# A decoder step in fp32: spacing out the scan's activation and moving the first row tile's products

## Chip, cores and metric

One Trainium2 chip, one core. The time is microseconds of the device for one execution of the whole program; lower is better. TensorE (PE) does matrix products, PEld is its loading of weights, VectorE (DVE) and ScalarE (ACT) work element by element, GpSimd (POOL) and SyncE (SP) here issue transfers and little else. "line" numbers such as L905 are those of the kernel before; in the kernel after, the same code stands some lines lower.

## What is computed

One layer of a decoder for 304 rows (16 meta tokens, 256 prompt tokens, 8 x 4 sample tokens), width 2048, all in float32:

```python
x = x + 0.5 * swiglu(rmsnorm(x), ffn1)          # hidden 5632
z = rmsnorm(x) @ w_in                           # 2048 -> 1024 + 1024 + 2048 + 2048
a = pool_mix(z[:, :1024])                       # sliding means over 2, 4, 8, 16 rows, minus identity, then pool_w
s = gelu(s5_scan(z[:, 1024:2048]))              # 64 groups of 16 channels, 64 complex states each
s = s * sigmoid(s @ glu_w + glu_b)
m = sigmoid(gate_a) * (a @ w_branch_a) + sigmoid(gate_b) * (s @ w_branch_b)
x = x + m @ w_out
x = x + 0.5 * swiglu(rmsnorm(x), ffn2)
y = rmsnorm(x)
```

The scan is linear: bu = u times a complex matrix per group, then h[t] = lam * h[t-1] + bu[t], then the real part of h times a matrix, plus d * u. The gelu behind it is written as y * sigmoid(c * (y * y + k) * y).

## The kernel before

**Products and weights.** Each weight is split into a high and a low part (`whi` by ACT, `wlo` by DVE), each activation too, and each product is three matmuls (`mm3`, L249 to L251). Weights come in chunks of 512 KB on SP's queue, one chunk per step of `proj`: 24 matmuls for a chunk, then `step`. `step` makes the high part of a later chunk (`high`), runs what was posted for this place (`flush`), makes the low part, loads the next chunk, and then advances the side work: a generator that yields after each small step, `g.rate` steps per chunk (2.25 during the scan). So the program order on every engine follows from where in the chunks the side steps fall. Each engine runs its own queue in that order.

**PSUM.** Four banks serve the projections, three (`psaux`) the side work in turn, one (`pslong`) the scan's output and, at the start, some products.

**The mixer.** `w_in` is run in eight column pairs, in the order `COLS`: pairs 0 to 3 feed the pool mix (`Pool.run`, side work), pairs 4 to 7 are the scan's input u, the ssm projections. Then `mixed` multiplies by `pool_w`, then come eight gate and `w_branch_a` projections, then eight more gate projections. The scan runs as side work beside all of this.

**The scan.** `Scan.run` goes through eight row tiles i, each in two halves h of twelve steps n (`rows`, all DVE: products with the tables `ee`, two scans, products again). For a tile, `into` makes bu: one matmul of the stacked input `us` (high, low, high part) with `bs`, then a copy by ACT from the bank to a `row` tile; twelve matmuls and copies per tile, two per call. The calls for tile i + 1 are spread over tile i at steps 5, 8, 11, 14, 17 and 20, counted over both halves. For the first tile all twelve are made at the start of `run`, in three side steps. `stored` writes the split input to memory (`usc`), `stacked` reads it back as `us`, `matrices` reads `bs` and `cs`; all these are issued on POOL's queue, and `us` and `bs` have one buffer each, so a read waits for the products of the tile before. `outof` (step 3) makes the output `yps` of the tile before, and `act` its gelu: gy = d * u + yps (DVE), square (ACT), gw (DVE), sigmoid (ACT), gy * gw (DVE), the high part of it (ACT) and the low part (DVE).

In `run`, the gelu of the tile before is a generator that is advanced after the steps 6, 7 and 8:

```python
yield 1
if acts is not None and n >= 6 and next(acts, None) is None:
    acts = None
```

Of the kernel before, what the change touches and what calls it, by code (L numbers as in the profile page):

```python
# [10 lines left out]
F32 = mybir.dt.float32  # L11
F32R = mybir.dt.float32r
I32 = mybir.dt.int32
AF = mybir.ActivationFunctionType
ALU = mybir.AluOpType
# [27 lines left out]
JB = 2  # L43
# [4 lines left out]
LATE = 8  # L48
STIR = 9
LAG = 0  # L50
COLS = (0, 1, 2, 4, 3, 5, 6, 7)
ROWS = 12
MAGIC = 12582912.0
# [158 lines left out]
def vcol(g, name, i):  # L212
    c = VROWS[name][0] + i
    return g.vec[:, c:c + 1]
# [628 lines left out]
class Scan:  # L843
# [76 lines left out]
    def act(self, i):  # L920
        g, nc = self.g, self.g.nc
        y = g.act.tile([P, NT], F32, tag="acc", name=nm(g, "gy"))[:, :NL]
        w = g.act.tile([P, NT], F32, tag="gw", name=nm(g, "gw"))[:, :NL]
        nc.vector.scalar_tensor_tensor(y, self.u[i][:, NMETA:], vcol(g, "ssm_d", i), self.yps[i], ALU.mult, ALU.add)
        nc.scalar.activation(w, y, AF.Square)
        yield 1
        nc.vector.scalar_tensor_tensor(w, w, 1.0 / 0.044715, y, ALU.add, ALU.mult)
        nc.scalar.activation(w, w, AF.Sigmoid, scale=2.0 * 0.044715 * math.sqrt(2.0 / math.pi))
        yield 1
        nc.vector.tensor_tensor(y, y, w, ALU.mult)  # L930
        self.sparts.append(split(g, y, NL, "Y"))
        yield 1

    def rows(self, sb, s):

# [41 lines left out]
    def first(self):  # L977

        self.matrices(0)
        self.pair = [self.load(0), self.load(1)]  # L980

    def run(self):
        half = 4 // JB
        nb = NJ // JB
        pair = self.pair
        for ri in (2, 1, 0):
            for h in range(half):
                self.into(0, pair, ri, h, h == half - 1)
            yield 1
        self.stored(1)  # L990
        self.stacked(1)
        self.matrices(1, outs=False)
        done, acts = None, None
        for i in range(KW):
            nxt = [dict(bu={}) for _ in range(half)]
            for h in range(half):
                sb = i * half + h
                rows = self.rows(sb, pair[h])
                if sb >= 1 and sb + 1 < nb:
                    new = self.load(sb + 1)  # L1000
                    (nxt[0] if h else pair[1])["ee"] = new["ee"]
                for n, row in enumerate(rows):
                    row()
                    if h == 0 and n == 3 and done is not None:
                        self.outof(i - 1, done)
                        acts = self.act(i - 1)
                    if h == 0 and n == 8 and i + 1 < KW:
                        self.matrices(i + 1, ins=False)
                    k, late = divmod(h * len(rows) + n - 5, 3)
                    if i + 1 < KW and late == 0 and 0 <= k < 6:  # L1010
                        self.into(i + 1, nxt, 2 - k % 3, k // 3)
                    if h == 0 and n == 2 and i + 2 < KW:
                        self.stored(i + 2)
                    if h and n == 9 and i + 2 < KW:
                        self.stacked(i + 2)
                        self.matrices(i + 2, outs=False)
                    yield 1
                    if acts is not None and n >= 6 and next(acts, None) is None:
                        acts = None
            done, pair = pair, nxt  # L1020
        self.outof(KW - 1, done)
        yield 1
        yield from self.act(KW - 1)

    def store(self, O, sp):
        g, nc = self.g, self.g.nc
# [85 lines left out]
def mixer(g, norm, O, ps0):  # L1112
# [14 lines left out]
    with ExitStack() as cm:  # L1127
        g.mix = cm.enter_context(g.tc.tile_pool(name="mix", bufs=1))
        with ExitStack() as cs:
            sp = cs.enter_context(g.tc.tile_pool(name="scan", bufs=1))  # L1130
            scan = Scan(g, sp)
            pool = Pool(g, O)
            dparts, aparts = [], []
            g.side, g.rate = None, POOLRATE
            for p in COLS:
                if p < KW // 2:
                    pool.fetch(p)
                ps = proj(g, "w_in", p * 256, norm.x, NT, KD) if p else ps0
                if p < KW // 2:
                    more = lambda p=p, ps=ps: also(g, pool.run(p, ps, norm, dparts))  # L1140
                    g.post.append(more if p else lambda more=more: g.post.append(more))
                else:
                    g.post += [lambda q=q: scan.input(q, norm.r) for q in ps]
                if p == 1:
                    scan.first()
                if p == KW // 2 - 1:
                    nc.gpsimd.dma_start(O[3][0, :, :HIST - NS], g.I["state_pool"][0, :, NS:])
                if p == KW // 2 + 1:
                    drain(g)
                    g.side, g.rate = scan.run(), MIXRATE  # L1150
                    g.owed = -LAG * MIXRATE
            def mixed():
                for q in range(4):
                    if q % 2:
                        flush(g)
                    else:
                        wh, wl = g.w.take("pool_w", 2 * q, 4, 0)
                    for f in range(2):
                        ps = bank(g, "pw")[:, :NL]
                        for k in range(2):  # L1160
                            fs = slice(f * P, (f + 1) * P)
                            kk = 2 * (q % 2) + k
                            mm3(g, ps, wh[:, kk, fs], wl[:, kk, fs], dparts[2 * q + k], k == 0, k == 1)
                        g.post.append(lambda i=2 * q + f, ps=ps: aparts.append(
                            split(g, ps, NL, "Y", vcol(g, "pool_scale", i))))
                    if q % 2:
                        step(g)

            mixed()
            for p in range(KD // 2):  # L1170
                pg = proj(g, "w_in", 2 * WP + p * 256, live, NL, KD)
                z = []
                g.post.append(lambda: z.extend(gate(pg[f], 2 * p + f) for f in range(2)))
                pa = proj(g, "w_branch_a", p * 256, aparts, NL, KW)

                def gated(p=p, z=z, pa=pa):
                    for f in range(2):
                        nc.vector.tensor_tensor(z[f], pa[f], z[f], ALU.mult)
                        nc.sync.dma_start(msc[2 * p + f], z[f])

                g.post.append(gated)
            for p in range(KD // 2):
                pg = proj(g, "w_in", 2 * WP + D + p * 256, live, NL, KD)

                def gated(p=p, pg=pg):
                    for f in range(2):
                        nc.sync.dma_start(gsc[2 * p + f], gate(pg[f], KD + 2 * p + f))

                g.post.append(gated)
            flush(g)  # L1190
            drain(g)
# [206 lines left out]
```

## Time and profile before

| what | us |
|---|---|
| median of 3 runs (lowest, highest) | 2351.66 (2351.46, 2353.5) |
| the profiled execution, its own time | 2350.9 |
| its span, first to last instruction | 2349.0 |
| PE busy | 2321.2 |
| DVE busy | 1584.3 |
| ACT busy | 967.9 |
| mixer from the first scan product to the last (bu, L905) | 979.9 to 1260.2 |

A matmul's time in the trace overlaps that of the next one, so the busy time of PE says how long it was supplied, and the distance between starts says how fast it ran. A row of the timeline has start, duration, engine, line, operation, output and inputs, how many like it follow, and in brackets how long the engine was idle before and who ended that. The stretches by time have the granted clock of PE as a share of full speed.

### The profile page before, as it was taken

The numbers are of one execution on the slowest core, as the hardware profiler recorded it, in microseconds if no ns is written. First come the engines' busy times: TensorE is split into PE (matmuls) and PEld (weight loads), VectorE is DVE, ScalarE is ACT, GpSimd is POOL, SyncE is SP. The second block draws the span as 40 slices with busy tenths as digits, with TensorE's granted clock in tenths as the row PEclk, the third lists the DMA queues.
The fourth block names the chain that finished last, engine by engine and source line by source line (L and its number), as shares of the span: only waits on it lengthen the run. The fifth ranks groups of instructions, "written<-read, shape, count | busy, mean of one in ns | idle before, by whom it ended". The sixth has DMA issues, their size and how long they took to land.

```text
span 2349.0 us, 41939 instructions
## 1 busy us (share of the span) xinstructions
PE 2321.2 (99%) x17177; PEld 2307.5 (98%) x17177; DVE 1584.3 (67%) x2414; ACT 967.9 (41%) x1382; POOL 130.5 (6%) x240
## 2 busy tenths in 40 slices
PE   9999999999999999999999999999999999999998
PEld 9999999999999999899999999999999999999997
DVE  7788777877554567689999765555554655555555
ACT  6333433333333345454445444343333333333334
POOL 0000000002200002211110130000000000000000
PEclk9999999999999999999999999999999999999999
DMA  6445555556754446667785575444444444444443
GB/s 227 161 152 194 188 206 204 206 191 204 207 188 153 162 168 224 195 201 254 235 264 209 204 261 173 162 168 165 165 168 165 165 168 167 162 171 163 169 163 112
DMA packets 133296, 438.32 MB, mean 187 GB/s; under 512 B 22036, under 2 KB 34624, under 8 KB 133096
## 3 DMA queue, kind: packets, MB, share of 16 engines
q1 hardware_dynamic: 106944, 374.35, 46.3%
q0 software_dynamic: 25872, 61.10, 8.6%
q8 instruction: 135, 2.21, 0.4%
q14 instruction: 57, 0.47, 0.1%
q10 hardware_dynamic: 288, 0.19, 0.0%
HBM read 403.45 MB, written 32.47 MB: 186 GB/s over the span
## 4 chain that ended last, share of the span: by engine, by line
PE 92%; DVE 4%; DMA 2%; ACT 1%; issue 1%; POOL 0%; SPq 0%; ACTq 0%; DVEq 0%; POOLq 0%
PE pj L250 22%; PE pj L249 22%; PE pj L251 22%; PE dn L251 8%; PE dn L249 8%; PE dn L250 8%; DVE wlo L171 1%; DMA raw<-in_w_in 1%; DVE row L938 1%; ACT whi L162 0%; DVE row L961 0%; PE yps L917 0%; PE bu L905 0%; ACT row L906 0%; DMA bs<-bsc 0%
## 5 line engine op out<-in xcount | busy, mean ns | idle before, releaser
L171 DVE TENSOR_TENSOR wlo<-raw,whi 128x1024 fp32r<-128x1024 f32 x695 | 849.2, 1223 | 582.5 <-ACT whi L162 578.5
L162 ACT CAST whi<-raw 128x1024 fp32r<-128x1024 f32 x695 | 729.9, 1051 | 1175.4 <-PE pj L250 677.8
L249 PE MATMUL pj<-X,whi 128*128 128x304 f32 (+1 forms) x2432 | 731.2, 301 | 1.5 <-DVE Y L278 1.3
L250 PE MATMUL pj<-X,whi 128*128 128x304 f32 (+1 forms) x2432 | 730.0, 300 | 0.0
L251 PE MATMUL pj<-X,wlo 128*128 128x304 f32 (+1 forms) x2432 | 729.7, 300 | 0.0
L250 PE MATMUL pj<-Y,whi 128*128 128x288 f32 x1728 | 510.3, 295 | 0.0
L249 PE MATMUL pj<-Y,whi 128*128 128x288 f32 x1728 | 509.4, 295 | 0.0
L251 PE MATMUL pj<-Y,wlo 128*128 128x288 f32 x1728 | 509.3, 295 | 0.0
L249 PEld LDWEIGHTS pj<-X,whi 128*128 128x128 f32 x2432 | 458.7, 189 | 4.0 <-DVE Y L278 1.5
L251 PEld LDWEIGHTS pj<-X,wlo 128*128 128x128 f32 x2432 | 457.8, 188 | 0.7 <-DVE wlo L154 0.4
L250 PEld LDWEIGHTS pj<-X,whi 128*128 128x128 f32 x2432 | 458.2, 188 | 0.0
L249 PEld LDWEIGHTS pj<-Y,whi 128*128 128x128 f32 x1728 | 325.2, 188 | 1.0 <-issue 0.9
L250 PEld LDWEIGHTS pj<-Y,whi 128*128 128x128 f32 x1728 | 325.0, 188 | 0.0
L251 PEld LDWEIGHTS pj<-Y,wlo 128*128 128x128 f32 x1728 | 324.5, 188 | 0.0
L251 PE MATMUL dn<-H,wlo 128*128 128x304 f32 x704 | 213.0, 303 | 0.0
L249 PE MATMUL dn<-H,whi 128*128 128x304 f32 x704 | 212.8, 302 | 0.0
L250 PE MATMUL dn<-H,whi 128*128 128x304 f32 x704 | 212.2, 301 | 0.0
L250 PE MATMUL dn<-X,whi 128*128 128x288 f32 x704 | 207.7, 295 | 0.0
L249 PE MATMUL dn<-X,whi 128*128 128x288 f32 x704 | 207.5, 295 | 0.0
L251 PE MATMUL dn<-X,wlo 128*128 128x288 f32 x704 | 207.4, 295 | 0.0
L250 PEld LDWEIGHTS dn<-H,whi 128*128 128x128 f32 x704 | 132.4, 188 | 0.0
L250 PEld LDWEIGHTS dn<-X,whi 128*128 128x128 f32 x704 | 132.4, 188 | 0.0
(262 smaller groups left out, 1868.2 us busy)
## 6 DMA issues: line engine op xcount, KB each, us to landing
raw<-in_ffn_w_down SPq DMA_DIRECT2D x176, 512.0 KB, 3.3
raw<-in_ffn_w_gate SPq DMA_DIRECT2D x175, 512.0 KB, 3.3
raw<-in_ffn_w_up SPq DMA_DIRECT2D x175, 512.0 KB, 3.3
raw<-in_w_in SPq DMA_DIRECT2D x96, 512.0 KB, 4.2
raw<-in_w_out SPq DMA_DIRECT2D x32, 512.0 KB, 3.9
esc<-ee POOLq DMA_DIRECT2D x16, 912.0 KB, 5.7
ee<-esc POOLq DMA_DIRECT2D x16, 912.0 KB, 7.1
raw<-in_w_branch_a SPq DMA_DIRECT2D x16, 512.0 KB, 3.4
```

Source lines behind the costliest of these rows:

```text
L162: self.g.nc.scalar.copy(hi, self.raw[i])
L171: self.g.nc.vector.tensor_tensor(lo, raw, hi.bitcast(F32), ALU.subtract)
L249: mm(ps, wh, x[0], start=start, stop=False)
L250: mm(ps, wh, x[1], start=False, stop=False)
L251: mm(ps, wl, x[0], start=False, stop=stop)
L938: scan = lambda o, f, x: nc.vector.tensor_tensor_scan(fl(o), fl(f), fl(x), 0.0, ALU.mult, ALU.add)
```

## The change

Three things are changed. First, the gelu of a row tile is a list of seven pieces, each with the step (0 to 23, over both halves) behind which it is issued: 6, 8, 9, 11, 12, 14, 15. Where `into` stands at the same step, the piece is issued after the product and its copies. Second, `begin` makes the products of the first row tile inside the second ssm projection (pair 5), ahead of its chunks 1, 2 and 3; ahead of chunk 0 it stores the second tile's input, and with chunk 3 it issues the reads of the second tile's `us` and `bs`. `run` no longer does this, so the scan starts three side steps further on. Third, `mixed` takes three side steps off what is owed.

```diff
+MIXLAG = 3
@@ class Scan @@
     def act(self, i):
         y, w = ...
-        nc.vector.scalar_tensor_tensor(y, self.u[i][:, NMETA:], vcol(g, "ssm_d", i), self.yps[i], ALU.mult, ALU.add)
-        nc.scalar.activation(w, y, AF.Square)
-        yield 1
-        nc.vector.scalar_tensor_tensor(w, w, 1.0 / 0.044715, y, ALU.add, ALU.mult)
-        nc.scalar.activation(w, w, AF.Sigmoid, scale=...)
-        yield 1
-        nc.vector.tensor_tensor(y, y, w, ALU.mult)
-        self.sparts.append(split(g, y, NL, "Y"))
-        yield 1
+        stt = nc.vector.scalar_tensor_tensor
+        hi, lo = part(g, "Y", NL), part(g, "Y", NL)
+        self.sparts.append((hi, lo))
+        return [(6, lambda: stt(y, self.u[i][:, NMETA:], vcol(g, "ssm_d", i), self.yps[i], ALU.mult, ALU.add)),
+                (8, lambda: nc.scalar.activation(w, y, AF.Square)),
+                (9, lambda: stt(w, w, 1.0 / 0.044715, y, ALU.add, ALU.mult)),
+                (11, lambda: nc.scalar.activation(w, w, AF.Sigmoid, scale=scale)),
+                (12, lambda: nc.vector.tensor_tensor(y, y, w, ALU.mult)),
+                (14, lambda: nc.scalar.copy(hi, y)),
+                (15, lambda: nc.vector.tensor_tensor(lo, y, hi.bitcast(F32), ALU.subtract))]
+    def begin(self, c):
+        if c == 0:
+            self.stored(1)
+            return
+        for h in range(4 // JB):
+            self.into(0, self.pair, 3 - c, h, bool(h))
+        if c == 3:
+            self.stacked(1)
+            self.matrices(1, outs=False)
     def run(self):
-        for ri in (2, 1, 0):
-            for h in range(half):
-                self.into(0, pair, ri, h, h == half - 1)
-            yield 1
-        self.stored(1)
-        self.stacked(1)
-        self.matrices(1, outs=False)
...
+                    while acts and h * len(rows) + n >= acts[0][0]:
+                        acts.pop(0)[1]()
                     yield 1
-                    if acts is not None and n >= 6 and next(acts, None) is None:
-                        acts = None
@@ mixer @@
-                ps = proj(g, "w_in", p * 256, norm.x, NT, KD) if p else ps0
+                before = scan.begin if p == KW // 2 + 1 else None
+                ps = proj(g, "w_in", p * 256, norm.x, NT, KD, before) if p else ps0
...
             def mixed():
+                g.owed -= MIXLAG
```

How the order moves, at three places. In the rows, `pj` and `pw` are banks of projections, `bu` the bank of a scan product, `ph` and `po` banks of the pool mix's transposes, X and Y the split activations.

PE behind the first chunk of the third ssm projection (pair 6), before: all of the first tile's products but four.

```order
L251 MATMUL pj_10883<-X_9596,wlo_10787 128x304
L905 MATMUL bu_10919<-us_10615,bs_10245 128x304
L905 MATMUL bu_10922<-us_10615,bs_10245 128x304
L905 MATMUL bu_10926<-us_10615,bs_10245 128x304
L905 MATMUL bu_10929<-us_10615,bs_10245 128x304
L905 MATMUL bu_10933<-us_10615,bs_10245 128x304
L905 MATMUL bu_10936<-us_10615,bs_10245 128x304
L905 MATMUL bu_10940<-us_10615,bs_10245 128x304
L905 MATMUL bu_10943<-us_10615,bs_10245 128x304
L249 MATMUL pj_10882<-X_9643,whi_10825 128x304
```

After, PE behind the first chunk of the second ssm projection (pair 5), 96 matmuls earlier:

```order
L252 MATMUL pj_10717<-X_9596,wlo_10651 128x304
L1080 MATMUL ph_10756<-ident,hist_10577 128x120 x2
L906 MATMUL bu_10768<-us_10615,bs_10245 128x304
L906 MATMUL bu_10771<-us_10615,bs_10245 128x304
L906 MATMUL bu_10775<-us_10615,bs_10245 128x304
L906 MATMUL bu_10778<-us_10615,bs_10245 128x304
L250 MATMUL pj_10716<-X_9643,whi_10679 128x304
```

The products go to a place behind the pool mix's transposes, four at a time instead of eight.

DVE beside the pool mix's products (`pw`), before. Y is the low part of what `pw` gives, and with it the bank is free; u is the scan's last input.

```order
L859 TENSOR_TENSOR u_11269<-pj_11089,rs_y_10147 128x304
L278 SCALAR_TENSOR_TENSOR Y_11272<-pw_11253,vec,Y_11271 128x288
L278 SCALAR_TENSOR_TENSOR Y_11276<-pw_11260,vec,Y_11275 128x288
L278 SCALAR_TENSOR_TENSOR Y_11296<-pw_11279,vec,Y_11295 128x288
L278 SCALAR_TENSOR_TENSOR Y_11300<-pw_11286,vec,Y_11299 128x288
L171 TENSOR_TENSOR wlo_11303<-raw_11154,whi_11293 128x1024
L938 SCALAR_TENSOR_TENSOR row_10939<-d_1658_11237,row_10939 128x608
L968 TENSOR_TENSOR row_10983<-row_10983,ee_10253 128x608
L278 SCALAR_TENSOR_TENSOR Y_11324<-pw_11309,vec,Y_11323 128x288
L278 SCALAR_TENSOR_TENSOR Y_11328<-pw_11316,vec,Y_11327 128x288
```

After, the same place:

```order
L279 SCALAR_TENSOR_TENSOR Y_11307<-pw_11290,vec,Y_11306 128x288
L279 SCALAR_TENSOR_TENSOR Y_11311<-pw_11297,vec,Y_11310 128x288
L172 TENSOR_TENSOR wlo_11314<-raw_11166,whi_11304 128x1024
L279 SCALAR_TENSOR_TENSOR Y_11333<-pw_11318,vec,Y_11332 128x288
L279 SCALAR_TENSOR_TENSOR Y_11337<-pw_11325,vec,Y_11336 128x288
L279 SCALAR_TENSOR_TENSOR Y_11357<-pw_11340,vec,Y_11356 128x288
L279 SCALAR_TENSOR_TENSOR Y_11361<-pw_11347,vec,Y_11360 128x288
L172 TENSOR_TENSOR wlo_11364<-raw_11211,whi_11354 128x1024
L941 SCALAR_TENSOR_TENSOR row_10885<-d_1652_11177,row_10885 128x608
```

No step of the scan stands between the Ys any more; the scan instruction comes behind the mix.

ACT in the sixth row tile, with the gelu of the fifth, before (`gw<-gy` is the square, `gw<-gw` the sigmoid, `d` the scan's factors):

```order
L162 CAST whi_13492<-raw_13356 128x1024
L925 ACTIVATE gw_13503<-gy_13502 128x288
L928 ACTIVATE gw_13503<-gw_13503 128x288
L906 COPY row_13512<-bu_13513 128x304
L906 COPY row_13512<-bu_13516 128x304
L162 CAST whi_13543<-raw_13409 128x1024
L274 CAST Y_13550<-gy_13502 128x288
L906 COPY row_13558<-bu_13559 128x304
L906 COPY row_13558<-bu_13562 128x304
L162 CAST whi_13589<-raw_13454 128x1024
L947 ACTIVATE d_2053_13595<-hc,rdec 128x304 x2
```

After:

```order
L907 COPY row_13511<-bu_13515 128x304
L930 ACTIVATE gw_13426<-gy_13425 128x288
L163 CAST whi_13543<-raw_13409 128x1024
L907 COPY row_13554<-bu_13555 128x304
L907 COPY row_13554<-bu_13558 128x304
L932 ACTIVATE gw_13426<-gw_13426 128x288
L163 CAST whi_13586<-raw_13458 128x1024
L950 ACTIVATE d_2053_13592<-hc,rdec 128x304 x2
L163 CAST whi_13624<-raw_13505 128x1024
L907 COPY row_13632<-bu_13633 128x304
L907 COPY row_13632<-bu_13636 128x304
L934 CAST Y_13427<-gy_13425 128x288
```

Each of ACT's three pieces now stands behind a pair of copies from `bu`, and a pair of copies stands between them.

On POOL's queue two `usc` writes move ahead of two writes `out<-up` of the pool mix, and the reads of `us` and `bs` for the second tile follow those. SP's queue is the same.

## What I predict

> **What bounds the kernel now.** I read the page's engine totals first, then the waits of the matmul engine, then its rows in order of time around each wait, and last the stretches by clock.
>
> ```profile
> span 2349.0 us, 41939 instructions
> PE 2321.2 (99%) x17177; PEld 2307.5 (98%) x17177; DVE 1584.3 (67%) x2414; ACT 967.9 (41%) x1382; POOL 130.5 (6%) x240
> ```
>
> PE is busy for 99% of the span, so only time in which PE stands still, or runs slowly, can be won. The waits of PE (who waited for whom: total us, times, longest) say where it stands:
>
> ```profile
> PE bu L905 <- ACT row L906: 7.1, 6, 2.2
> PE bu L905 <- DMA bs<-bsc: 5.9, 1, 5.9
> PE pj L249 <- DVE Y L278: 1.3, 1, 1.3
> PE pw L249 <- DVE u L859: 0.5, 1, 0.5
> ```
>
> All four lie in the scan or just ahead of it. PE in order of time (start, us, xcount, idle before):
>
> ```profile
> 979.91 2.16 PE L905 MATMUL bu<-us,bs 96*128 96x304 f32 x8
> 981.91 0.30 PE L249 MATMUL pj<-X,whi 128*128 128x304 f32 x1
> ...
> 998.57 0.84 PE L905 MATMUL bu<-us,bs 96*128 96x304 f32 x2 [5.91 <-DMA bs<-bsc]
> ...
> 1002.46 0.30 PE L250 MATMUL pj<-X,whi 128*128 128x304 f32 x1
> 1002.60 0.30 PE L251 MATMUL pj<-X,wlo 128*128 128x304 f32 x1
> ...
> 1203.17 0.31 PE L905 MATMUL bu<-us,bs 96*128 96x304 f32 x1
> 1205.55 0.41 PE L905 MATMUL bu<-us,bs 96*128 96x304 f32 x1 [2.07 <-ACT row L906]
> ```
>
> Undisturbed matmuls last 0.30 us and start 0.14 apart (1002.46, 1002.60), so a wait shown as idle x costs x + 0.16. How PE ran behind these waits is read from stretches of time (PE busy and count first, then PEld, DVE, ACT, POOL, then the granted clock):
>
> ```profile
> 998.50:1002.30 3.80, 3.73 (x15) 3.76 (x16) 1.40 (x2) 1.67 (x3) 0.00 (x0) 0.50 0.49 167
> 1024.00:1250.00 226.00, 218.89 (x1702) 210.77 (x1700) 208.85 (x304) 111.94 (x196) 33.50 (x63) 1.00 0.76 241
> ```
>
> The granted clock is 0.50 behind that wait: 15 matmuls take 3.8 us instead of 2.1, a loss of 1.7. In the stretch with the six short waits it is 1.00, so they cost their length alone. What PE loses: (a) the wait for bs, 5.9 + 0.16 = 6.1; (b) the slow clock, 1.7; (c) the eight first-tile products, 981.91 - 979.91 = 2.0 for eight of 0.14, 0.9; (d) pw, 0.7; (e) the first gate projection behind Y, 1.4; (f) six waits for the copies of bu, 7.1 + 6 x 0.16 = 8.1. Together 18.9 us, the most the change can win.
>
> [...]
>
> **The first row tile's products, moved into the second ssm projection (c, and the cover for a and b).** Twelve matmuls and twelve copies move, none is added. They now stand behind its first, second and third chunk of weights, four each. The first four are reached at 966.1 or so:
>
> ```profile
> 966.12 0.37 PE L1070 MATMUL ph<-ident,hist 120*128 120x120 f32 x2
> 966.53 0.42 ACT L1072 COPY pt<-ph 128x120 f32<-128x120 f32 x2 [2.59 <-PE ph L1070]
> 973.44 0.37 ACT L1106 COPY up<-po 47x256 f32<-47x256 f32 x1 [1.22 <-PE po L1104]
> 985.61 1.36 ACT L906 COPY row<-bu 128x304 f32<-128x304 f32 x4 [1.79 <-PE bu L905]
> ...
> L896 POOL DMA_DIRECT2D us<-usc x6: 542/556/567, 953.6 to 991.4; - x6
> DMA to landing us min/median/max: 4.2/4.5/5.9
> ```
>
> Their operand us is issued in three parts from 953.6, each 0.56, so the last starts at about 955 and, with the slowest landing shown, is there at 961: 5 us to spare. Four products use three shared PSUM banks and the long one; ph has just taken one of the three, so the third product waits until ACT has copied ph (966.95) and loses about 0.4; the third group does the same behind po. That is 0.8 for the 0.9 of (c): 0.1 gained. Four copies take ACT 1.36 us per chunk of 24 x 0.14 = 3.4 us, where it stood idle for 2.59 and 1.22 us in the two gaps shown. The casts of weights behind them come about a microsecond later; they run whole chunks ahead of PE, which is why none of PE's large waits is for whi. If that lead were gone, each late copy would cost PE its 1.36 us.
>
> **The second tile's transfers (a, b).** Now they are issued at the end of that projection:
>
> ```profile
> 974.10 0.54 POOL L1108 DMA_DIRECT2D out<-up  x1 [17.95 <-ACT up L1106]
> 974.65 0.59 POOL L1109 DMA_DIRECT2D out<-up  x1
> 987.60 0.56 POOL L889 DMA_DIRECT2D usc<-uhi  x1 [12.36 <-ACT uhi L886]
> 990.30 1.65 POOL L896 DMA_DIRECT2D us<-usc  x3 [1.60 <-DMA usc<-uhi]
> 991.94 1.49 POOL L876 DMA_DIRECT2D bs<-bsc  x3
> ...
> L876 POOL DMA_DIRECT2D bs<-bsc x6: 497/511/524, 921.2 to 992.9; - x6
> DMA to landing us min/median/max: 4.4/5.0/5.5
> ```
>
> The two usc writes move ahead of out<-up and so past its wait of 17.95 us for ACT; they now run a whole projection ahead of the reads. On POOL's queue the reads of us and bs stand behind out<-up and wait until the last first-tile product has read the old us. By my count that is at 976: 966.3 behind ph, two chunks of 3.4, three groups of 0.56, 0.3 for po and the 0.8 above. Then come up to 1.1 of issue for out<-up, 1.65 and 1.49: the last bs starts at about 979.7 and lands by 985.2. PE needs it behind the third chunk of the next projection, which starts at 976 + 3.4 = 979.4; three chunks on it is 989.6. The margin is 4.4 us, so (a) and (b) go whole: 7.8. If the cover fails, they come back. Behind these reads on POOL's queue stand the third tile's usc writes and the second's cs, which are read only a row tile later.
>
> **The pool mix without side steps (d, e).** DVE in order of time there:
>
> ```profile
> 1016.59 0.85 DVE L859 TENSOR_TENSOR u<-pj,rs_y 128x304 f32<-128x304 f32 x2
> ...
> 1021.10 1.42 DVE L938 TENSOR_TENSOR_SCAN row<-d,row 128x608 f32<-128x608 f32 x1
> 1022.43 0.77 DVE L968 TENSOR_TENSOR row<-row,ee 128x608 f32<-128x608 f32 x1
> 1023.12 1.79 DVE L278 SCALAR_TENSOR_TENSOR Y<-pw,vec,Y 128x288 fp32r<-128x288 f32 x4
> ```
>
> A scan and a product, 2.0 us from start to start, stand ahead of the Y that frees the banks PE waits for; they go behind it. Y then ends about 2 us earlier against a wait of 1.4: I take 1.2. The scan itself runs three steps earlier until then, since its first three are gone, so DVE has less left to do when it reaches u, and I take 0.6 of (d). Were DVE late all the same, (d) and (e) would stay as they are: 1.8 back. Behind the mix the steps stand at the same chunk as before, so the three skipped steps cost nothing at the scan's end.
>
> **Gelu in seven pieces (f).** The longest wait, on ACT and DVE:
>
> ```profile
> 1203.71 0.44 ACT L925 ACTIVATE gw<-gy 128x288 f32<-128x288 f32 x1 [4.29 <-DVE gy L924]
> 1204.75 0.44 ACT L928 ACTIVATE gw<-gw 128x288 f32<-128x288 f32 x1 [0.59 <-DVE gw L927]
> 1205.10 0.71 ACT L906 COPY row<-bu 128x304 f32<-128x304 f32 x2
> 1212.49 0.73 ACT L906 COPY row<-bu 128x304 f32<-128x304 f32 x2 [0.25 <-PE bu L905]
> 1203.17 0.51 DVE L924 SCALAR_TENSOR_TENSOR gy<-u,vec,yps 128x288 f32<-128x288 f32 x1
> 1206.79 1.23 DVE L171 TENSOR_TENSOR wlo<-raw,whi 128x1024 fp32r<-128x1024 f32 x1 [1.40 <-ACT whi L162]
> 1209.25 0.75 DVE L973 TENSOR_TENSOR row<-row,ee 128x576 f32<-128x576 f32 x1
> ```
>
> ACT stands in square and sigmoid until DVE has made gy and gw, and the copies that PE needs (1205.10) are queued behind. Now those copies come first. The next copies stand behind the square: gy ends at 1203.7, square 0.44, copies 0.71, so 1204.9. The product that needs their bank comes just ahead of 1212.49, less the 2.2 us that PE no longer loses: 1210, 5 us of margin. The copies after them stand behind the sigmoid, which needs the row at 1209.25 and gw: at most 1210.0 + 0.45 + 0.44 = 1210.9, if DVE were no faster than before. Those copies (1212.49, less 2.2) would then be 0.6 us late, for a product one chunk, 3.4 us, further on. I keep 0.6 of (f) for such places: 7.5 gained. A bound from both sides: nothing of (f) stays, or all of it.
>
> Does DVE keep up? From 1024 to 1250 it works 208.85 us; PE needs 226 - 8.1 = 217.9. Nine us are left, and its waits for ACT there (1.40 above) shrink too.
>
> The sum: 7.8 + 0.1 + 0.6 + 1.2 + 7.5 = 17.2. The profiled execution took 2350.9 us (span 2349.0, 1.9 around it), so 2333.7; the median of the runs, 2351.66, is 0.8 above it: **2334.5**.
>
> **Rivals.** One: the wait only moves. ACT stays one queue in order, and the sigmoid and the cast of Y now stand ahead of the copies two and three products later; DVE is busy for 92% of that stretch, and if it falls another 5 us behind, (f) returns: 2334.5 + 7.5 = 2342.0. [...] For it speaks the sigmoid that may be 0.6 us late; against it, the chunk of 3.4 us behind it and 9 us of DVE time left over. Chance 0.13.
>
> Two: us and bs land too late after all, a 5 us slip on POOL's queue; (a) and (b) return, 2342.3. The one landing window known, 4.4 to 5.5, speaks against it. Chance 0.05.
>
> Three: both, so that the change does not do what it says: 2349.8, no change. Chance 0.04.
>
> Four, the slower side: the first products stand in a projection that PE ran through without a wait, and their own us is not there yet. PE comes there at 966.1, and would lose the 17.2 again if it landed at 983.3, 28 us after its issue at 955; at 33 us the time is 2334.5 + 21.9 + 1.7 of clock = 2358.1. The slowest of six landings took 5.9. Chance 0.03.
>
> **How the numbers follow.** My forecast has 0.75, and by itself reaches from 2332.5 (all 18.9 won, 2332.8) to 2338 (the 1.7 that I let stay, three times as large). The range of 2332.5 to 2342.5 takes in the first two rivals. Faster by over 0.2%, the least that a measurement of this kernel can tell from no change, here 4.7 us: 0.75 + 0.13 + 0.05 = 0.93; same 0.04; slower 0.03.
>
> **What would show it.** Right: no wait of bu for bs and no stretch at clock 0.50 near 1000; bu in groups of four from 966; bu's wait for the copies below 1 us in total; Y and u gone from PE's waits. Wrong: bu waiting for the copies behind the sigmoid or z; PE waiting for wlo, the sign that DVE is the bound; a wait of bu for us inside the projection.

## The result and the profile after

The changed kernel takes 2333.93 us (median of 4 runs, 2333.62 to 2334.41), the kernel before in the same session 2351.56. The ratio is 0.9924, 95% interval 0.9906 to 0.9941. The forecast was 2334.5.

The page of the changed kernel, its span and engine totals, and the waits of PE in and ahead of the scan (total, times, longest); three more, of 0.6 to 1.1 us, stand at the very start and end of the program, where nothing was changed:

```profile
span 2332.6 us, 41945 instructions
PE 2317.6 (99%) x17177; PEld 2307.1 (99%) x17177; DVE 1584.4 (68%) x2414; ACT 968.3 (42%) x1382; POOL 130.4 (6%) x240
```

```profile
PE pw L250 <- DVE u L860: 1.3, 1, 1.3
PE bu L906 <- ACT pt L1082: 0.2, 1, 0.2
PE bu L906 <- ACT up L1116: 0.2, 1, 0.2
```

DVE, ACT and POOL are busy as long as before; PE stands still less. The waits of `bu` for `bs` and for the copies (`row`), and of the gate projection for `Y`, are gone. One has grown: `pw` for `u`, 0.5 before and 1.3 now. The two small waits of `bu` are new; they are the first tile's products waiting for PSUM banks.

Two stretches of time of the same profile (length, then PE, PEld, DVE, ACT, POOL, granted clock):

```profile
990.00:1000.00 10.00, 10.00 (x74) 10.00 (x73) 9.86 (x14) 4.41 (x7) 0.00 (x0) 1.00 0.45 147
1008.00:1234.00 226.00, 224.71 (x1756) 218.00 (x1756) 216.66 (x316) 120.68 (x210) 34.05 (x64) 1.00 0.78 249
```

Where PE had stood 5.91 us and then run at 0.50, it runs through at 1.00. In the scan, 226 us now hold 1756 matmuls instead of 1702, and DVE is busy for 216.66 of them; before, it was busy for 208.85 of the 226 us from 1024 to 1250. DVE is now idle for only 9.3 us there.

The reads of `bs` came in time with less to spare than forecast. The last of the second tile's three was issued at 980.9 and, with the longest landing shown, was there at 988.8; PE came to the product at 990.55:

```profile
L877 POOL DMA_DIRECT2D bs<-bsc x3: 529/539/539, 979.9 to 980.9; - x3
DMA to landing us min/median/max: 6.9/6.9/7.9
```

The prediction had taken 5.5 us for the slowest landing and so a margin of 4.4 us. The margin was 1.8.

For all runs below I give one more number beside the time. From the start of the 285th group of 24 weight products (`pj`, `pw` and, in the feed-forward, `dn`) to that of the 380th, every kernel does the same products, and opening and end of the kernel are left out. This stretch takes 352.31 us before and 334.51 after, 17.8 less. The profiled times differ by 16.5 only (2350.9 and 2334.41), because this one execution after the change reached its 21st group 1.3 us later (76.61 against 75.32), before anything that was changed.

A stretch is read from one execution of each kernel. The runs of the kernel before lie between 2350.45 and 2357.05, and the profiled one, 2350.9, is among the fastest; those of the change lie within 0.8. So what a stretch is "less than before" can be 1 to 2 us too small.

### The profile page after: what moved, and what is told of

It reads as the page before. It is cut to its first block, busy times and chain, and to the rows that moved or that the text cites. A ratio compares the mean times of both kernels' runs of the same rounds, so it can differ in the third digit from the quotient of the medians.

```text
span 2332.6 us, 41945 instructions
## 1 busy us (share of the span) xinstructions
PE 2317.6 (99%) x17177; PEld 2307.1 (99%) x17177; DVE 1584.4 (68%) x2414; ACT 968.3 (42%) x1382; POOL 130.4 (6%) x240
## 4 chain that ended last, share of the span: by engine, by line
PE 98%; DVE 1%; ACT 0%; DMA 0%; issue 0%; ACTq 0%; SPq 0%; DVEq 0%
PE pj L251 24%; PE pj L250 24%; PE pj L252 24%; PE dn L252 8%; PE dn L250 8%; PE dn L251 8%; PE bu L906 1%; PE yps L918 1%; DMA raw<-in_ffn_w_gate 0%; DVE acc L339 0%; PE ss L349 0%; DVE wlo L172 0%; ACT y L1295 0%; PE ty L1257 0%; PE rb L365 0%
```

## Experiments

All were timed in three rounds beside the kernel before. The sessions' medians of before were 2351.56, 2353.22, 2352.70 and 2352.70, so kernels of different sessions are compared by the stretch.

**Each part alone: the products moved.** `begin` is kept; the gelu has its three bundles again, and no steps are skipped.

```diff
-MIXLAG = 3
+MIXLAG = 0
@@ act, run: the generator of the kernel before @@
```

> The first part of the change alone: the second tile's first products stand inside the last projection but three of the pool mix's layer, its transfers go out there; the activation stays in three bundles and the pool mix keeps its side steps. Theory (the terms of the prediction add up): the wait of bu for bs (6.1) and the slow clock behind it (1.7) go, the products' own bank waits cost what they save (0.1), the six waits for ACT's copies (8.1) stay: 2351.6 - 7.9 = 2343.7, ratio 0.9966. The two waits in the pool mix (0.7 and 1.4) stay. Rival, the parts hang together (with fewer steps owed, DVE comes to the pool mix later): part of it is given back in pw's wait for u, which grows from 0.7 by 1 us or more, 2344.5 to 2346. Rival, the reads are late without the rest of the change: 2351.

(The products that move are the first row tile's, into the second ssm projection; only the reads are the second tile's.)

Measured: 2346.18 (2345.07 to 2347.68), ratio 0.9970 (0.9957 to 0.9983), stretch 345.87, 6.4 less than before. Waits of PE:

```profile
PE bu L906 <- ACT row L907: 5.9, 5, 2.5
PE pw L250 <- DVE u L860: 1.3, 1, 1.3
PE yps L918 <- DVE row L974: 1.1, 1, 1.1
```

The wait for `bs` and the slow clock went whole, as forecast. But the first rival of this run holds: `pw`'s wait for `u` grew from 0.5 to 1.3 with this part alone, and a new wait stands at the scan's end (`yps` for `row`). So the growth of `u` in the changed kernel is made by this part. It is not because PE no longer stands for `bs` and leaves DVE less time: in `late_long` below, PE stands 9.3 us for it and the wait for `u` is 1.3 all the same.

**The gelu alone.**

```diff
-MIXLAG = 3
@@ begin is not there; run issues the first tile's products and transfers as before @@
```

> The second part alone: square, sigmoid, product and cast of each pair's output handed out in seven spaced pieces behind the copies. Theory: the six waits go whole, 8.1 by the waits alone; the difference of the two traces in that stretch is 9.35, so 2351.6 - 8.1 to 9.4 = 2342.2 to 2343.5, ratio 0.9960 to 0.9966. Rival one of the prediction, the wait only moves to the copies behind the sigmoid, or DVE becomes the bound: some of it returns, 2346 to 2351. The bs wait and the clock at 0.50 behind it must still be there in both.

Measured: 2343.51 (2343.12 to 2343.85), ratio 0.9956 (0.9941 to 0.9971), stretch 344.89, 7.4 less. Waits of PE, and ACT in order of time at the one that is left:

```profile
PE bu L905 <- DMA bs<-bsc: 6.0, 1, 6.0
PE bu L905 <- ACT row L906: 1.4, 1, 1.4
```

```profile
1088.09 0.96 ACT L1129 ACTIVATE z<-z,vec 128x288 f32<-128x288 f32 x2 [2.56 <-DVE z L1128]
1088.96 0.70 ACT L906 COPY row<-bu 128x304 f32<-128x304 f32 x2
```

Five of the six waits are gone. The sixth, as long as before (1.4), now has another cause: ACT stands 2.56 us in the gate's activation `z`, which waits for DVE, and the copies are behind it. That is rival one in small. In the changed kernel this place is not late: ACT stands 1.23 us for `z` there, and PE does not wait. The first part shifts the scan against the projections, which would do this; no run tests it alone.

**The pool mix alone.**

```diff
+MIXLAG = 3
 def mixed():
+    g.owed -= MIXLAG
```

> The third part alone: the pool mix skips three side steps; nothing else is changed. Theory of the prediction: pw's wait for u loses 0.6 and pj's wait for Y loses 1.2: 2351.6 - 1.8 = 2349.8, ratio 0.9992. Rival, from the trace of the changed kernel, where pw's wait grew: only Y's wait goes, 1.2 to 1.4, and u's stays at 0.7 or more: 2350.2 to 2350.6. A further rival: steps skipped here are owed to the scan and come back as a wait at its end: 2351.6 or above.

Measured: 2350.39 (2347.46 to 2351.75, 10 runs), ratio 0.9984 (0.9975 to 0.9993), stretch 351.82, 0.5 less. Its waits, and the clock behind the one for `bs`:

```profile
PE bu L906 <- DMA bs<-bsc: 6.2, 1, 6.2
PE bu L906 <- ACT row L907: 5.5, 6, 1.7
PE pw L250 <- DVE u L860: 0.5, 1, 0.5
```

```profile
999.50:1005.50 6.00, 6.00 (x24) 6.00 (x25) 3.32 (x3) 1.67 (x3) 0.00 (x0) 0.50 0.51 169
```

`Y`'s wait is gone and `u`'s is unchanged, as the second reading had it: the skip does nothing for `u`. That the stretch gained only 0.5 has to do in part with the clock. It stayed at 0.50 for 6 us behind much the same wait that was followed by 3.8 us in the kernel before; 24 matmuls in 6.0 us are 2.6 us lost instead of 1.7. The last section says why.

The three parts alone take 6.4, 7.4 and 0.5 from the stretch, 14.3 in sum; together they take 17.8. By the medians, each against the kernel before in its session, they take 7.0, 9.7 and 2.8, 19.6 in sum, and together 17.6. So whether they are worth more together is not shown. What the traces do show is that single waits of a part run alone (`yps` for `row`, 1.1; the copies behind `z`, 1.4) are not there in the whole. The next runs look at the waits around the mix.

**All but the skip, and the skip moved.** `mix_none` has no skip, `mix_early` skips three steps ahead of the last chunk of the last ssm projection instead, `mix_six` skips there and in the mix. Of `mix_early` and `mix_six`:

```diff
                 before = scan.begin if p == KW // 2 + 1 else None
+                if p == KW - 1:
+                    def before(c):
+                        if c == 3:
+                            g.owed -= 3
@@ mix_none and mix_early @@
-MIXLAG = 3
+MIXLAG = 0
```

> The changed kernel without its third part (no side steps skipped in the pool mix). Theory, from the first part run alone: pw's wait for u stays at 1.3 to 1.4, for the earlier start of the second tile's products makes it; pj's wait for Y (1.4) comes back, and so does the wait of yps for row at the scan's end (1.8 of PE there): 2333.9 + 1.4 + 1.8 = 2337.1. Rival, the spaced pieces leave DVE the time for the scan's end: only Y's wait, 2335.3. Rival, the prediction's terms (0.6 of u and 1.2 of Y): 2335.7, with u's wait larger than with the skip.

> The changed kernel with the three steps skipped ahead of the last chunk of the last projection before the pool mix, and none in the mix. Theory (u is late because DVE still works on the scan and on wlo when pj is done): three steps less, some 3 us of DVE, ahead of u, so pw's wait of 1.44 falls to below 0.5; with the steps of the mix back, Y's wait may return with up to 1.4: 2332.9 to 2334.3. Rival (DVE stood idle 2.02 us for whi from ACT just ahead of u, and the steps have nothing to do with it): u's wait stays, Y's returns, 2335.3.

> The changed kernel with three more steps skipped ahead of the last chunk of the last projection before the pool mix, besides the three in it. Theory: pw's wait for u falls from 1.44 to below 0.5, Y's stays away, and the scan, now six steps behind, still ends in time: 2333.9 - 1.0 = 2332.9. Rival (DVE's idle 2.02 us for whi from ACT sets u): 2333.9. Rival (six steps are too many): a wait at the end of the scan, or DVE falls behind, 2335 or more.

Measured, on one chip: 2336.44 (2335.42 to 2336.83), 2334.24 (2333.85 to 2334.62) and 2332.21 (2331.91 to 2333.45); stretches 337.64, 334.83 and 333.26, against 334.51 with the change as it is. Waits of PE in the first; in the second, `Y`'s alone is left of these, with 1.4:

```profile
PE pj L250 <- DVE Y L279: 1.4, 1, 1.4
PE pw L250 <- DVE u L860: 1.3, 1, 1.3
PE yps L918 <- DVE row L976: 0.4, 1, 0.4
```

DVE ahead of `u` in the kernel before, where `u` started at 1016.59:

```profile
1014.14 0.78 DVE L964 TENSOR_TENSOR row<-row,ee 128x608 f32<-128x608 f32 x1
1014.84 0.78 DVE L965 TENSOR_TENSOR row<-row,ee 128x608 f32<-128x608 f32 x1
1015.66 0.79 DVE L961 TENSOR_TENSOR row<-row,row 128x608 f32<-128x608 f32 x1
```

In the changed kernel, and then with six steps skipped:

```profile
1004.06 1.23 DVE L172 TENSOR_TENSOR wlo<-raw,whi 128x1024 fp32r<-128x1024 f32 x1 [2.02 <-ACT whi L163]
...
1008.10 1.42 DVE L941 TENSOR_TENSOR_SCAN row<-d,row 128x608 f32<-128x608 f32 x1
1009.44 0.77 DVE L971 TENSOR_TENSOR row<-row,ee 128x608 f32<-128x608 f32 x1
1010.24 0.79 DVE L964 TENSOR_TENSOR row<-row,row 128x608 f32<-128x608 f32 x1
...
1011.17 0.84 DVE L860 TENSOR_TENSOR u<-pj,rs_y 128x304 f32<-128x304 f32 x2
```

```profile
1003.19 1.23 DVE L172 TENSOR_TENSOR wlo<-raw,whi 128x1024 fp32r<-128x1024 f32 x1 [2.05 <-ACT whi L163]
...
1007.30 0.89 DVE L860 TENSOR_TENSOR u<-pj,rs_y 128x304 f32<-128x304 f32 x2
```

Steps of the scan stand ahead of `u` in both kernels: 2.45 us of them before (1014.14 to 1016.59), 3.07 in the changed kernel (1008.10 to 1011.17), where one is a scan of 1.42 and not a product of 0.78. The difference, 0.6, is near the 0.7 by which the wait grew. Taken away, `u` comes at 1007.30 and `pw`'s wait is gone, although DVE still stands 2.05 us for `whi`: the rival that this idle time sets `u` falls. `mix_early` trades `u`'s wait for `Y`'s, `mix_six` has neither. It is the lowest time of all the runs: its stretch is 1.25 below that of the change, its median 1.7 below (not timed beside each other, and the intervals of their ratios to before overlap). Without any skip the stretch is 3.1 longer than with the skip in the mix: 1.5 of it is `Y`'s wait and below 1 that of `yps` at the scan's end; the rest is spread over the scan. So, by this one pair of traces, the skip gives more than the wait of `Y` for which it was counted.

**Order against spacing.** Is it that the pieces stand behind the copies, or that they are spaced? Two runs change one each. In `gelu_ahead` the pieces stand ahead of the copies of the same step; in `gelu_three` behind them, but in three bundles.

```diff
@@ gelu_ahead, in run @@
+                    while acts and h * len(rows) + n >= acts[0][0]:
+                        acts.pop(0)[1]()
...
-                    while acts and h * len(rows) + n >= acts[0][0]:
-                        acts.pop(0)[1]()
@@ gelu_three, in act: square (8), sigmoid (11) and hi (14) keep their steps @@
-        return [(6, lambda: stt(y, ...
+        return [(8, lambda: stt(y, ...
-                (9, lambda: stt(w, ...
+                (11, lambda: stt(w, ...
-                (12, lambda: nc.vector.tensor_tensor(y, ...
+                (14, lambda: nc.vector.tensor_tensor(y, ...
-                (15, lambda: nc.vector.tensor_tensor(lo, ...
+                (14, lambda: nc.vector.tensor_tensor(lo, ...
```

> The changed kernel with one order turned: each of the seven pieces stands ahead of the input copies of its step instead of behind them; the steps are the same. Theory A, the spacing does it (by the time ACT comes to a piece its operand is there, so that a piece costs the copies behind it only its own 0.44): no change, 2333.9 to 2334.5. Theory B, standing behind the copies does it (ACT's queue is in order, and a piece that waits for DVE holds the copies): the waits of bu for ACT's copies come back in part, 4 to 9 us, 2338 to 2343.

> The changed kernel with the seven pieces still behind the input copies, but in three bundles as the kernel before had them (row product and square; second product and sigmoid; product and both casts), at steps 8, 11 and 14. Theory A, the order on ACT's queue is all that matters: 2333.9 to 2334.5. Theory B, the spacing matters as well (ACT comes to a square or sigmoid whose operand DVE has yet to make, stands there, and the next copies, two or three products later, are late): 1 to 5 us of waits of bu for the copies come back, 2335 to 2339.

Measured: `gelu_ahead` 2336.78 (2336.39 to 2336.95), stretch 336.82, 2.3 more than the change, between what the two theories gave. `gelu_three` 2355.01 (2353.51 to 2357.03), slower by 0.1% than the kernel before (ratio 1.0011, 1.0002 to 1.0021), stretch 357.45, 22.9 more. ACT at the same pair's sigmoid, in the changed kernel and then in `gelu_ahead`:

```profile
1193.71 0.45 ACT L932 ACTIVATE gw<-gw 128x288 f32<-128x288 f32 x1 [0.70 <-DVE gw L931]
...
1198.91 0.73 ACT L907 COPY row<-bu 128x304 f32<-128x304 f32 x2 [1.99 <-PE bu L906]
```

```profile
1196.93 0.45 ACT L932 ACTIVATE gw<-gw 128x288 f32<-128x288 f32 x1 [3.49 <-DVE gw L931]
1197.28 0.71 ACT L907 COPY row<-bu 128x304 f32<-128x304 f32 x2
...
1206.24 0.96 ACT L1134 ACTIVATE z<-z,vec 128x288 f32<-128x288 f32 x2 [2.94 <-DVE z L1133]
```

In the change ACT is ahead: it waits for PE's product (1.99), not PE for it. Ahead of the copies, the sigmoid holds them for 3.49 us, and from then on ACT runs late; PE paid 1.39 at the copies behind `z`. In `gelu_three`, ACT at a square, DVE's waits for ACT from 1008 to 1234, and the largest waits of PE in the scan:

```profile
1161.43 0.45 ACT L930 ACTIVATE gw<-gy 128x288 f32<-128x288 f32 x1 [4.87 <-DVE gy L929]
```

```profile
DVE wlo L172 <- ACT whi L163: 19.2, 16, 2.8
```

```profile
PE bu L906 <- ACT row L907: 5.7, 3, 2.2
PE pj L250 <- DVE z L1133: 5.0, 3, 2.1
PE yps L918 <- DVE row L977: 1.8, 1, 1.8
```

DVE reached the product of a step after ACT had come to the same step: here ACT stood from 1156.56, and DVE began `gy` at 1160.89, 4.3 us later. In a bundle ACT therefore stands, 4.87 us here and 2.77 at the sigmoid behind it. I read the rest as a loop: the casts `whi` behind the piece come late, DVE stands for those (19.2 us in all instead of 5.9 in the change), and then what DVE makes is late, `z`, the next piece, and at last `row`. No run cuts this loop to test it. Three of PE's waits were also followed by a granted clock of 0.50 for 3.41 us each, 1.7 us lost in each, about 5 of the 22.9 us.

Theory B holds for `gelu_three`, but far above its price of 1 to 5: I had counted the copies that come late. Two limits belong to it. First, 22.9 is the price at steps 8, 11 and 14: the kernel before had the same three bundles, at the steps 6, 7 and 8, and there their waits cost about 9. Second, the distance alone does not keep ACT from standing. From 1008 to 1234 ACT stands 27.3 us at the three pieces before, 44.4 in `gelu_three`, 25.3 in `gelu_ahead` with the full distance, and 2.6 only in the change, where the copies ahead of a piece make ACT wait for PE first (53.0 us for the products of `bu`, 22.6 before). PE pays for little of the 25.3; no run shows why.

**The reads of us and bs put back.** In `late_long` the products stay and only the reads go back behind the third tile's `usc` writes; in `late_short` they go between these two writes, `bs` first.

```diff
@@ begin @@
         if c == 3:
-            self.stacked(1)
-            self.matrices(1, outs=False)
@@ run; late_short: inside stored, behind its first write @@
                         self.stored(i + 2)
+                        if i == 0:
+                            self.stacked(1)
+                            self.matrices(1, outs=False)
```

> The changed kernel with the second tile's reads of us and bs put back on POOL's queue to where the kernel before issued them, behind the writes of the third tile's usc; the products stay where the change has them. Theory: the wait of bu for bs is back with 6 to 6.5 us, and behind it a stretch of some 4 to 7 us with the granted clock at about 0.50, which costs 1.7: 2333.9 + 7.7 to 8.2 = 2341.6 to 2342.1, so that the place of the reads is the whole gain of the first part. Rival (the products' earlier start is what gained it): 2334 to 2336.

> The changed kernel with the second tile's reads, bs first and us behind it, put on POOL's queue between the two writes of the third tile's usc: a few us earlier than where the kernel before issued them. Theory: the last bs starts at about 986 to 987, lands 5 to 9 us later, so bu waits 2.2 to 5.5 us. The question is the clock behind a wait of that length: six waits of up to 2.2 us in the kernel before were followed by a clock of 1.00, one of 5.9 by 0.50 for some 3 us, one of 9.35 (reads put later still) by 0.50 for 5 to 6 us. If the length of the wait sets it, a wait of 2 to 3 us brings no slow clock or one below 1 us, and the time is 2333.9 plus the wait, 2336 to 2339; if each wait above some 2 us brings the whole slow stretch, 1.7 more.

Measured: 2345.94 (2345.82 to 2346.72) and 2342.10 (2341.79 to 2342.41); stretches 12.4 and 7.0 above the change. PE's wait, POOL's queue and the clock behind the wait in the first; the wait in the second, which the clock followed at 0.50 as well:

```profile
PE bu L906 <- DMA bs<-bsc: 9.3, 1, 9.3
```

```profile
987.15 0.54 POOL L890 DMA_DIRECT2D usc<-ulo  x1 [1.88 <-DVE ulo L888]
...
989.34 1.49 POOL L877 DMA_DIRECT2D bs<-bsc  x3
```

```profile
999.20:1004.70 5.50, 5.50 (x22) 5.50 (x23) 3.21 (x3) 1.67 (x3) 0.00 (x0) 0.50 0.19 43
```

```profile
PE bu L908 <- DMA us<-usc: 4.6, 1, 4.6
```

Between the two rows of POOL stand the reads of `us`. The place of the reads is the whole gain of (a) and (b), as the theory had it; the products' own place gains nothing. The wait is longer than I forecast, for two reasons: PE comes to the product 2.9 us earlier than in the kernel before (989.8 and 992.7), and the last `bs` starts at about 990.3 and PE goes on at 999.1, so it took nearly 9 us to land where the profile before showed 5. In `late_short` it was `us`, now issued last, that PE waited for.

**More work for DVE.** 32 and 64 extra sums whose results nothing reads, each 0.46 long by the profile.

```diff
@@ dve_more @@
+                    if n in (1, 7):
@@ dve_most @@
+                    if n in (1, 4, 7, 10):
@@ both @@
+                        x = self.sp.tile([P, 1], F32, ...)
+                        self.g.nc.vector.reduce_sum(x, self.g.hc[:, :NT], axis=mybir.AxisListType.X)
```

> The changed kernel with two extra sums on DVE (128x304 to 128x1, about 0.4 each) in each half of a pair of the scan, 32 in all, some 13 us more for DVE, whose results nothing reads. DVE is idle for 9.3 us of the 226 from 1008 to 1234. Theory (DVE is close to the bound and the change has used up its room): 13 us more eat the 9.3 and the rest shows, with PE waiting for wlo, row or for copies held behind DVE's pieces: 2336 to 2340. Rival (DVE runs ahead of PE with room in its buffers and the steps behind the pool mix): 2334 to 2335.

> As the run with two extra sums in each half, with four: 64 in all, some 26 us more for DVE. Theory: DVE is now the bound of that stretch, and all beyond its idle time shows: 26 less 9.3 is 17, so 2345 to 2351. Rival (idle time outside 1008 to 1234 takes it up, some 1 us in 4 being idle behind it): 2336 to 2340.

Measured: 2341.78 (2341.19 to 2343.06) and 2350.10 (2347.46 to 2354.48); stretches 6.9 and 17.5 above the change. The first lies above the range of its theory, the second within. Waits of PE in the first, and the whole stretch in the changed kernel and in the two runs (the third busy time is DVE's):

```profile
PE bu L906 <- ACT row L907: 3.4, 2, 2.9
PE yps L918 <- DVE row L977: 1.2, 1, 1.2
```

```profile
964.11:1298.62 334.51, 332.82 (x2576) 323.40 (x2574) 309.51 (x458) 173.89 (x300) 41.33 (x78) 1.00 0.74 235
964.28:1305.71 341.43, 334.40 (x2576) 323.54 (x2574) 319.35 (x490) 172.04 (x300) 41.30 (x78) 1.00 0.75 230
963.39:1315.39 352.00, 339.73 (x2576) 327.42 (x2574) 329.91 (x523) 172.91 (x300) 41.34 (x78) 0.99 0.74 224
```

The sums do not add 0.46 each, but 0.31 and 0.32: DVE is busy for 9.8 and 20.4 us more. By my estimate it is because each overlaps its neighbours, as the rows of DVE above do by 0.08 (0.78 from 1014.14 ends at 1014.92, the next starts at 1014.84); 0.08 at both ends makes 0.30 of 0.46. DVE's idle time is 25.0, 22.1 and 22.1 us. So only about 3 us of it took up sums, and all that was added beyond that shows in the time. The 9.3 idle us from 1008 to 1234 were not room: with the sums DVE is idle for 8.9 and 9.2 us there. In the first run the extra is paid for in waits of `bu` for ACT's copies and of `yps` for `row`, and not in waits of PE for `wlo`, which I had named as the sign. In the second, the granted clock of 0.50 behind two waits is about 4.6 of the 17.5.

## Why the prediction was right, and where its terms were not

The time, 2333.9 for 2334.5, came out by the forecast mechanism in its large terms: the wait for `bs`, the slow clock, the six waits for the copies and that for `Y` are gone, and no rival came true. That it came out within 0.6 us is luck: the terms below missed by up to 1.4 us, and the misses cancel. By terms, in the stretch, by the starts of PE's products:

- (a) and (b), won whole for 7.8: right, 7.6. The last read of `bs` started at 980.9 (forecast 979.7), and PE came to the product at 990.55 (forecast 989.6). But "lands by 985.2" was not so: the landing took up to 7.9 us, not 5.5, and with 1.8 us more the wait would have begun to come back. `begin_only` gave this part alone, and `late_long` took it back.
- (c), 0.1 for bank waits of 0.8: right within 0.2. The two waits cost 0.39 and 0.34, and in sum the move lost 0.1.
- (e), 1.2 for `Y`: right in cause, 1.8 measured.
- (d), 0.6 for `u`: wrong in sign. The loss went from 0.7 to 1.4. The step that failed is "the scan itself runs three steps earlier until then, since its first three are gone, so DVE has less left to do when it reaches u". The steps that the earlier start frees are not left out; others come up in their place, and those that then stood just ahead of `u` take 3.07 us instead of 2.45. The skip, which begins in the mix, comes behind them. `mix_only` shows that the skip leaves `u` alone, `begin_only` that the earlier start makes it worse, `mix_six` that three steps less ahead of it remove the wait.
- (f), 7.5 of 8.1: too small. All six waits are gone, the "0.6 late" sigmoid was not late (in the changed kernel the copies behind it wait 1.99 for PE), and the part with the six waits became 8.9 shorter (from 7.2 to 16.2 us ahead of before). Most of the 0.8 beyond the waits' own 8.1 is the first product behind each wait, which takes 0.41 instead of 0.31 (the rows at 1205.55 and 1203.17 before): 0.6 for six. A further 0.3 came at the scan's last output.

So (d) took back 1.3 of what I had counted, and (f) with (e) gave back 2.0. Rival one was the right thing to fear, but its place was not: at the distances chosen, ACT's order alone costs 2.3 (`gelu_ahead`), while the bundles at their new steps cost 22.9 (`gelu_three`). In the ACT rows above, the copies start behind the piece that stands ahead of them: in `gelu_ahead` the sigmoid stood 3.49 us and started at 1196.93, the copies at 1197.28. That the distance alone does not keep ACT from standing, `gelu_ahead` shows, 25.3 us against 27.3 before; spaced and behind the copies, the pieces stood for 2.6 us in all, and no wait of PE for the copies was left.

Of the nine us of DVE time "left over", 9.3 in the trace, the two runs with extra sums show that they are not room: about 3 us over the whole stretch took up sums. The change fits, but with less to spare than the prediction says.

## What to carry to other kernels

When an engine does pieces for which it needs another engine's result, and its queue runs in order as ACT's did in the rows above, look at two things: what each piece holds back in its own queue, and how far the producer lags at that place. Here pieces two steps behind their producer and behind the copies that PE needs brought PE no wait for a copy, the same pieces ahead of the copies cost 2.3 us, and pieces issued in the step of their producer 22.9 us at these places. A sigmoid that stood 3.49 us for its operand held the copies behind it, and where ACT stood most, 44.4 us at the pieces in `gelu_three`, DVE in its turn stood 19.2 us for ACT's casts. DVE's idle time was not its room: of 25 us in which it stood, some 3 took up extra work. Parts of a change that shift the same side work are not independent: the first part alone made `u`'s wait larger, and a step count that is skipped must be skipped ahead of the wait that it should relieve. Put a transfer's issue on its queue behind only what it must follow: the 9.3 us of one wait were the price of standing behind two writes.

## What the runs showed of the clock

I had taken it from one trace that waits of up to 2.2 us leave the granted clock at 1.00. That does not hold. Of the eleven waits of PE between 1.8 and 3.3 us in this part of the traces of all kernels here, five are followed by a clock of 0.50 to 0.66 in the next 1.5 us and six by 1.00; a longer one (2.93, `dve_more`) by 1.00 where a shorter (2.09, `gelu_three`) was not. All five of 4.6 us and more were followed by 0.50, and none below 1.8 us was. So the length of the wait does not tell.

Where the wait falls does, in these traces. In every one of the 14 traces the granted clock changes only at whole multiples of 3.41 us from its first change: in the kernel before it first changes at 5.69, falls at 995.55, which is 290 multiples on, and rises again at 1002.38, two more. Cut into windows at these times, with PE's busy time first and the granted clock third from the end, around the wait of 2.09 us in `gelu_three`:

```profile
1056.94:1060.35 3.41, 1.32 (x11) 1.07 (x9) 3.34 (x6) 0.25 (x2) 1.89 (x4) 1.00 0.66 177
1060.35:1063.76 3.41, 3.41 (x15) 3.41 (x16) 3.38 (x5) 3.35 (x6) 1.26 (x3) 0.50 1.26 249
```

Around that of 2.93 in `dve_more`, which an edge cut in two:

```profile
1205.18:1208.59 3.41, 1.98 (x15) 1.74 (x14) 3.34 (x6) 0.00 (x0) 0.00 (x0) 1.00 0.78 264
1208.59:1212.00 3.41, 1.91 (x14) 1.91 (x15) 3.34 (x7) 3.22 (x8) 1.21 (x3) 1.00 0.51 156
1212.00:1215.41 3.41, 3.41 (x28) 3.41 (x27) 3.38 (x4) 0.87 (x1) 1.92 (x4) 1.00 1.25 278
```

And the window that held most of the wait of 2.07 in the kernel before, behind which the clock stayed at 1.00:

```profile
1203.77:1207.18 3.41, 1.63 (x12) 1.64 (x13) 2.01 (x4) 2.39 (x5) 0.00 (x0) 1.00 0.43 156
```

From 950 to 1340 us this holds in all the traces: behind the ten full-speed windows in which PE was busy for 1.57 us or less the next window is at 0.50, and behind every one with 1.63 or more it is at 1.00. A slow window in which PE again stood for 0.55 us or more is followed by another slow one, one in which it did not stand at all by full speed. That is why the wait for `bs` brought two slow windows in the kernel before and three in `mix_only`: it ended 0.4 us ahead of an edge in the one and 0.7 behind an edge in the other. It also says what a fall to 0.50 cost here: up to 1.7 us, half a window, for each slow window that PE works through.

So 1.84 us of standing within one window (1.57 of work in 3.41) was enough for a fall here, and 1.78 (1.63 of work) was not. Why the clock changes at these times, no run shows.

The six waits of the kernel before all left the clock at 1.00, but not by much: the window with 1.63 us of work was the closest to a fall. The first change of the clock comes between 3.9 and 10.5 us in the 14 traces, so the windows lie differently in each. Other executions of that kernel may have had such falls and been slower for it; only one was traced, so this is not shown.
